# Shifts and scales of the first two quarters as products with w_ada as the stationary operand, and a new order of the first stage

## The chip, the cores and the metric

The kernel runs on one core of a Trainium2 chip, as one program. The metric is the device time of one execution in microseconds. Before the change it is 1251.24 us, the median of 3 runs (1251.12 to 1252.87). Engines go by the profile's names: PE (TensorE's matmuls), PEld (its weight loads), DVE (VectorE), ACT (ScalarE), POOL (GpSimd) and SP (SyncE, which issues most DMAs here).

## The reference, cut to what matters

One layer of a streaming encoder on 1024 prompt tokens and 32 sample tokens, D = 1024 channels. The first stage of the kernel computes this part:

```python
mod = jax.nn.silu(c) @ w_ada + b_ada            # c: one vector for the prompt, one for the samples
shift, scale, gate = jnp.split(mod, 3, axis=-1) # w_ada is 1024 x 3072
h = rms_norm(x, g_norm) * (1 + scale[:, None, :]) + shift[:, None, :]
z = h @ w_in                                    # all projections, 1024 x 8264
q, k, v, gate_a, iq, iw, ik, glu, gate_b, merge = split_in(z)
```

Behind it come an indexer that picks the top keys for each query, attention over those, a causal depthwise convolution of width 31, two output projections with gates, a last projection and a final norm. All of it is float32; the big products are made of three products of rounded halves (high x high, high x low, low x high).

## The kernel before, in words

The kernel runs through stages. The first one, which the change touches, makes h transposed: tiles hh and hl hold its high and low halves, with channels on partitions (8 blocks of 128 channels, j = 0 to 7) and 1056 tokens along the free axis. Beside it the stage computes the first index products: ik (the index keys and weights, 72 columns, in three pieces of 352 tokens: steps k:j,c) and the first 128 columns of iq (in two pieces, 512 and 288 tokens: steps q:j,c). When it ends, the projections follow (line 543 in helper proj, and the second iq product from line 132 on), 24 matmuls for each 128 columns and third of the tokens, which fill most of the span.

What the stage does in what order is written out by hand. LOADS lists the DMAs on SP's queue: x:i is token tile i (8 is the sample tile), a:g,h a block of w_ada for quarter g and half h of the rows (512 rows x 512 columns: the shifts and scales of two blocks of channels), k and q:0, q:1 the index weights. Tile pools limit them: three buffers for blocks of w_ada ("ada", line 228), six for x. A load that reuses a buffer waits on SP until its readers are done, and everything behind it in SP's queue waits too.

ORDER lists the steps of the compute engines; each engine goes through its own steps in this order. A last letter names the engine (D, P, A for DVE, POOL, ACT).

- sq, v, s, r, x: the norm of a token tile: sum of squares (ACT), variance (DVE), root (ACT), reciprocal and a correction (DVE), scaling of the tile in place
- t:i,q and c:i,q: four transposes of 128x128 on PE into a PSUM tile (misc, two buffers), and the copy to xT
- m:g,h (mod, line 339): products with a block of w_ada. Four matmuls; the stationary operand is the pair of vectors (padded to 32 columns), the 512 columns of w_ada move. The four go to four quarters of the output partitions: each has a fourth of the half's rows, and all accumulate over h
- a:g (mod_row, line 348): the PSUM tile is copied to SBUF; o:g (mod_cols, line 353): four transposes turn its rows to columns; O:g (mod_out, line 358): a reduce on DVE adds the four quarters, and bias and norm weight go on. After O:g the shifts and scales of blocks 2g and 2g + 1 stand in AB
- h:p,j, i:p,j, l:p,j: for part p of the tokens (f is tiles 0 and 1, i is 2 to 5, t is 6 and 7, tf is f and t) h in full, its high half (ACT) and the low half as their difference (DVE); S:g the same for the sample tokens
- wa, wd: the high and low halves of the index weights
- z:n: n matmuls of zeros, which fill PE's waiting time

Buffers and queues hold the steps together: mod of group 1 needs the blocks loaded into buffers that mod of group 0 has freed, and an index product of block j needs its h, which needs O of its quarter and the transposes of its tokens.

Of the kernel before, what the change touches and what calls it, by code (L numbers as in the profile page):

```python
# [24 lines left out]
OP = mybir.AluOpType  # L25
# [5 lines left out]
D = 1024  # L31
# [41 lines left out]
def steps(text):  # L73
    return [(op, *(int(v) if v.isdigit() else v for v in args.split(",") if v))
            for op, _, args in (word.partition(":") for word in text.split())]
# [3 lines left out]
x:8 x:2 x:3 x:4 x:5 a:0,0 a:0,1 k x:6 x:7 a:1,0 a:1,1 q:0 a:2,0 a:2,1 x:0 x:1 a:3,0 a:3,1 q:1  # L79
""")  # L80
ORDER = steps("""
sq:8 v:8 s:8 B sq:3 r:8 x:8,D s:3 sq:4 z:8 t:8,1 t:8,0 c:8,1,D v:3 c:8,0,D s:4 v:4 sq:5 r:4 x:4,D s:5 r:3 sq:2 z:5
t:4,0 v:5 t:4,1 x:3,P r:5 m:0,0 c:4,0,D s:2 c:4,1,A x:5,P v:2 t:3,0 r:2 c:3,0,A x:2,D z:1 t:5,1 t:2,0 c:5,1,D wa:k
c:2,0,D t:2,1 wd:k,P m:0,1 c:2,1,D sq:6 t:3,1 t:5,0 v:6 s:6 sq:7 r:6 a:0,D x:6,P s:7 v:7 c:3,1,A r:7 c:5,0,A z:5 o:0
O:0 t:6,1 c:6,1,A S:0,D h:i,0,P t:6,0 m:1,0 i:i,0 h:i,1,D x:7,P i:i,1 l:i,0 m:1,1 c:6,0,D l:i,1 k:0,1 wa:0 a:1,D
t:7,1 t:7,0 c:7,1,A wd:0,P k:1,1 c:7,0,A o:1 i:t,0 h:t,1,D O:1 m:2,0 i:t,1 h:t,0,D i:i,3 l:t,0 h:t,2,P q:0,0 l:t,1
h:i,2,P i:t,2 h:i,3,D k:0,2 i:i,2 l:i,3 q:1,1 S:1,P k:1,2 i:t,3 l:i,2 q:1,0 m:2,1 sq:0 q:3,0 s:0 v:0 sq:1 r:0 k:3,1
a:2,D x:0,P q:2,0 v:1 s:1 k:2,1 r:1 o:2 x:1,P t:0,0 O:2 m:3,0 c:0,0,A l:t,2 i:i,5 h:i,5,D S:2,P h:t,3,D t:1,0 i:i,4
l:t,3 t:0,1 c:1,0,D k:2,2 c:0,1,A m:3,1 l:i,5 h:i,4,P i:f,2 i:f,1 q:3,1 a:3,D h:f,3,P i:f,0 t:1,1 l:i,4 k:5,1 h:f,2,P
c:1,1,A q:5,0 i:tf,4 h:tf,4,D h:tf,5,P o:3 l:f,2 i:tf,5 k:4,1 O:3 k:2,0 S:3,P i:i,6 l:tf,5 q:4,0 i:i,7 l:tf,4 q:0,1  # L90
k:3,2 i:tf,7 q:2,1 k:5,0 i:f,3 k:5,2 i:tf,6 l:f,3 q:5,1 h:i,7,D k:4,2 h:i,6,P wa:1 k:4,0 l:i,7 q:4,1 h:tf,6,P l:i,6
k:3,0 q:7,0 h:f,0,P l:tf,6 q:6,0 wd:1,P l:f,0 k:7,1 h:tf,7,D k:6,0 l:tf,7 q:6,1 k:6,1 q:7,1 h:f,1,P k:7,0 k:7,2 l:f,1
k:0,0 k:6,2 k:1,0
""")

GROUPS = ((0, 2), (2, 2), (4, 2), (6, 2))


def pieces(n):
# [10 lines left out]
def _build(tc, nc, a, o, top):  # L110
# [10 lines left out]
    def tl(p, shape, dt, tag, bufs=1):  # L121
        return p.tile(shape, dt, name=tag, tag=tag, bufs=bufs)
# [49 lines left out]
    def misc(shape):  # L172
        return tl(psM, shape, F, "misc", 2)
# [48 lines left out]
    ada = {}  # L222
    xn = {}

    def load_ada(g, h):

        f, n = GROUPS[g]
        t = ada[g, h] = tl(stp, [128, 4, 512], F, "ada", 3)[:, :, :256 * n].rearrange("p k (i c) -> p k i c", i=2)
# [12 lines left out]
    for op, *i in LOADS:  # L241
# [6 lines left out]
        else:  # L248
            c = 128 * i[0]
# [16 lines left out]
    scp = tl(stp, [128, KD, 32], F, "scp")  # L266
# [70 lines left out]
    pm, mrow = {}, {}  # L337

    def mod(g, h):

        w = 256 * GROUPS[g][1]
        if h == 0:
            pm[g] = tl(psS, [128, 512], F, "acc")
        for j in range(4):
            nc.tensor.matmul(pm[g][32 * j:32 * j + 32, :w], scp[:, 4 * h + j, :],
                             ada[g, h][:, j].rearrange("p i c -> p (i c)"), start=h == 0, stop=h == 1)

    def mod_row(g, e):
        w = 256 * GROUPS[g][1]
        mrow[g] = tl(stp, [128, 512], F, "mrow")[:, :w]  # L350
        copy_on(e, mrow[g], pm.pop(g)[:, :w])

    def mod_cols(g):
        p = pm[g] = misc([128, 4, 128])
        for c in range(2 * GROUPS[g][1]):
            nc.tensor.transpose(p[:, c, :], mrow[g][:, 128 * c:128 * c + 128], ident)

    def mod_out(g):

        f, n = GROUPS[g]  # L360
        j = slice(f, f + n)
        mc = tl(stp, [128, 4, 2], F, "mc", 2)[:, :2 * n]
        nc.vector.tensor_reduce(out=mc, in_=pm.pop(g)[:, :2 * n].rearrange("p c (q s) -> p c s q", q=4)[:, :, 0:2],
                                axis=mybir.AxisListType.X, op=OP.add)
        bias = bg_[:, 0:16].rearrange("p (i j) -> p i j", i=2)[:, :, j, None]
        nc.vector.tensor_add(AB[:, j].rearrange("p j (i s) -> p i j s", i=2), mc.rearrange("p (i j) s -> p i j s", i=2),
                             bias.to_broadcast([128, 2, n, 2]))
        nc.vector.tensor_mul(AB[:, j, 2:4], AB[:, j, 2:4], bg_[:, 16:24][:, j, None].to_broadcast([128, n, 2]))
# [73 lines left out]
    def idle(n):  # L442

        for i in range(n):
            nc.tensor.matmul(ikp[:, 0, :], rest[:, 0:128], rest, start=True, stop=True)

    order = {"sq": sq_x, "v": var_x, "s": root_x, "r": over_x, "x": scale_x, "t": trans_x, "c": copy_x, "m": mod,
             "a": mod_row, "o": mod_cols, "O": mod_out, "h": h_of, "i": h_hi, "l": h_lo, "S": h_sample, "wa": w_hi,
             "wd": w_lo, "B": bias_out,
             "q": q_mm, "k": k_mm, "z": idle}  # L450
# [420 lines left out]
    def spill(dst, func):  # L871
        def f(j):
            def g(p):
                s = slot()
                nc.scalar.activation(c3(s[:, :T]), p[:, :, :CH], func)  # L875
                nc.scalar.dma_start(dst[128 * j:128 * j + 128, :], s[:, :T])
            return g
        return f
# [177 lines left out]
    def pairs(w, c0, f, rows):  # L1056
        return [("w", [(w, c0 + 128 * j, 256)], [(0, 128, f(j)), (128, 128, f(j + 1))], 1, rows)
                for j in range(0, KD, 2)]
# [225 lines left out]
    sq = [(u, r) for u in units for r in range(u.ns)]  # L1284
# [37 lines left out]
    def prelude():  # L1322
        more_q(1)
        more_g(2)
        for _ in range(8):
# [8 lines left out]
    m = (pairs(w_in, C_MA, spill(sma_d, AF.Sigmoid), hrows) + pairs(w_in, C_MB, spill(smb_d, AF.Sigmoid), hrows)  # L1334
         + pairs(w_in, C_GA, spill(ga_d, AF.Silu), hrows) + pairs(w_in, C_Q, spill_q, hrows))
# [111 lines left out]
    start = {}  # L1447
# [262 lines left out]
def _layout(x):  # L1710
# [10 lines left out]
    w = x["w_ada"][0]  # L1721
    for g, (f, n) in enumerate(GROUPS):
        for h in range(2):
# [25 lines left out]
```

## Time and profile before

| | us |
|---|---|
| time, median of 3 runs | 1251.24 (1251.12 to 1252.87) |
| the profiled execution's own time | 1251.41 |
| its span, from the first instruction to the last | 1249.6 |
| first stage, to the first projection's first matmul | 57.78 |
| last matmul | 1239.5 |

The span begins with the first instruction and the profile's times count from there. A row of a timeline gives start, length, engine, line, operation, output <- inputs, shapes and number of instructions merged, and in brackets the idle time before and what ended it. Matmuls of float32 operands appear as two records each; transposes and the matmuls of rounded halves as one. A chain of waits is followed back from the end, at each step to what released it.

### The profile page before, as it was taken

The page shows a single profiled execution, that of the slowest core. Times are in us where ns is not written, and L with a number is a line of the kernel's source. Part 1 is how long each engine was busy: PE and PEld are TensorE (multiplying, and loading weights), DVE is VectorE, ACT ScalarE, POOL GpSimd, SP SyncE. Part 2 cuts the span into 40 slices and gives each one's busy share as a digit, 9 for nine tenths or more (in the row PEclk, how much of TensorE's full clock was granted, in tenths as well). Part 3 has the DMA queues.
Part 4 walks back from the last instruction along what each step waited for, and adds up shares of the span by engine and source line. Part 5 has one row for each costly group of instructions (what it writes and reads, how often), then busy time and mean ns, then how long its engine had stood idle before and what let it go on. Part 6 is the DMA issues. An engine that isn't in the chain of part 4 may idle for free.

```text
span 1249.6 us, 18980 instructions
## 1 busy us (share of the span) xinstructions
PE 1229.2 (98%) x7403; PEld 1167.6 (93%) x7403; DVE 894.1 (72%) x1413; ACT 605.2 (48%) x1115; POOL 180.6 (14%) x279
## 2 busy tenths in 40 slices
PE   7999999999999999999999999999999999999996
PEld 3799999999999999999999999999998889999785
DVE  6766538988899888888876469752358888775464
ACT  6645545675666666671214343340247776123321
POOL 4610010000000000100000000000123352200343
PEclk8999999999999999999999999999999999999999
DMA  9412232213213113113223421276123336645422
GB/s 362 168 43 69 85 88 84 70 54 94 79 53 86 69 53 120 53 52 104 86 91 134 160 80 52 88 240 210 40 88 100 98 89 196 211 148 184 159 88 86
DMA packets 107898, 137.94 MB, mean 110 GB/s; under 512 B 9280, under 2 KB 88384, under 8 KB 106656
## 3 DMA queue, kind: packets, MB, share of 16 engines
q1 hardware_dynamic: 97136, 102.88, 25.9%
q10 hardware_dynamic: 5808, 19.06, 3.8%
q0 software_dynamic: 4864, 14.79, 3.6%
q8 instruction: 58, 0.95, 0.3%
q14 instruction: 32, 0.26, 0.1%
HBM read 100.43 MB, written 36.27 MB: 109 GB/s over the span
## 4 chain that ended last, share of the span: by engine, by line
PE 96%; DMA 1%; DVE 1%; ACT 0%; POOL 0%; issue 0%; SPq 0%; POOLq 0%; ACTq 0%
PE proj L543 70%; PE PT L1250 2%; PE y L132 2%; PE y L133 2%; PE y L134 2%; PE O L132 1%; PE O L134 1%; PE O L133 1%; PE misc L712 1%; PE misc L713 1%; PE misc L134 1%; PE misc L133 1%; PE misc L132 1%; DMA ada<-in_ada_dram 1%; PE proj L132 1%; PE proj L134 1%
## 5 line engine op out<-in xcount | busy, mean ns | idle before, releaser
L931 DVE SCALAR_TENSOR_TENSOR s<-u,vec,s 128x1086 f32<-128x1086 f32 x240 | 314.3, 1346 | 2.9
L543 PE MATMUL proj<-hl,wh 128*128 128x352 f32 x1440 | 311.6, 324 | 0.0
L543 PE MATMUL proj<-hh,wh 128*128 128x352 f32 x1440 | 311.3, 324 | 0.0
L543 PE MATMUL proj<-hh,wl 128*128 128x352 f32 x1440 | 309.0, 323 | 0.0
L543 PEld LDWEIGHTS proj<-hh,wh 128*128 128x128 f32 x1440 | 244.8, 188 | 1.6
L543 PEld LDWEIGHTS proj<-hh,wl 128*128 128x128 f32 x1440 | 246.0, 188 | 0.0
L543 PEld LDWEIGHTS proj<-hl,wh 128*128 128x128 f32 x1440 | 245.0, 188 | 0.0
L782 ACT ACTIVATE relu<-scores,cand 128x384 bf16<-128x384 f32 (+6 forms) x224 | 183.6, 821 | 82.2 <-DVE cand L797 78.5
L129 DVE TENSOR_TENSOR wl<-raw,wh 128x1024 fp32r<-128x1024 f32 (+1 forms) x82 | 97.8, 1195 | 71.1 <-ACT wh L128 71.0
L128 ACT CAST wh<-raw 128x1024 fp32r<-128x1024 f32 (+1 forms) x82 | 83.8, 1025 | 61.4 <-PE proj L543 49.3
L726 DVE SCALAR_TENSOR_TENSOR scores<-relu,iws,scores 128x384 f32<-128x384 f32 (+3 forms) x70 | 43.1, 655 | 31.6 <-ACT relu L715 31.5
L715 ACT ACTIVATE relu<-misc 128x384 f32<-128x384 f32 (+3 forms) x80 | 39.7, 523 | 52.4 <-PE misc L713 49.8
L128 ACT CAST u<-PT 128x512 fp32r<-128x512 f32 (+2 forms) x76 | 43.2, 572 | 44.5 <-PE PT L1250 42.2
L875 ACT ACTIVATE s<-proj 128x1056 f32<-128x1056 f32 x24 | 25.3, 1054 | 78.2 <-PE proj L543 78.2
L129 DVE TENSOR_TENSOR u<-PT,u 128x512 fp32r<-128x512 f32 (+2 forms) x76 | 50.6, 670 | 14.5 <-ACT u L128 14.2
L782 ACT ACTIVATION_READ_ACCUMULATOR relu<-scores,cand 128x1 f32 x224 | 42.0, 188 | 0.0
L543 PE MATMUL proj<-oa,wh 128*128 128x352 f32 x192 | 41.4, 323 | 0.0
L1230 POOL TENSOR_SCALAR E<-E,st 128x1024 f32<-128x1024 f32 (+4 forms) x36 | 33.6, 935 | 41.8 <-DVE st L1229 18.6
L543 PE MATMUL proj<-u,wh 128*128 128x352 f32 x192 | 38.7, 323 | 0.0
L1225 ACT ACTIVATE E<-E,st 128x1024 f32<-128x1024 f32 (+4 forms) x36 | 34.7, 963 | 8.1 <-DVE st L1218 7.9
L857 POOL DMA_DIRECT2D mask_d<-relu x7 | 3.8, 540 | 232.1 <-ACT relu L856 232.1
L885 DVE TENSOR_TENSOR s<-proj,s 128x1056 fp32r<-128x1056 f32 x8 | 10.1, 1256 | 35.6 <-ACT s L883 35.6
(400 smaller groups left out, 2052.1 us busy)
## 6 DMA issues: line engine op xcount, KB each, us to landing
raw<-in_w_in_dram SPq DMA_DIRECT2D x23, 1024.0 KB, 5.4
ada<-in_ada_dram SPq DMA_DIRECT2D x8, 1024.0 KB, 9.2
raw<-in_w_in_dram SPq DMA_DIRECT2D x16, 512.0 KB, 4.8
raw<-in_w_out_dram SPq DMA_DIRECT2D x6, 1024.0 KB, 5.4
sma_d<-s ACTq DMA_DIRECT2D x8, 528.0 KB, 2.7
smb_d<-s ACTq DMA_DIRECT2D x8, 528.0 KB, 2.8
ga_d<-s ACTq DMA_DIRECT2D x8, 528.0 KB, 2.7
qh_d<-s ACTq DMA_DIRECT2D x8, 528.0 KB, 2.7
```

The costliest lines, as they stand in the source:

```text
L128: nc.scalar.copy(hi, src)
L129: nc.vector.tensor_sub(lo, src, f32(hi))
L132: nc.tensor.matmul(out, ah, bh, start=first, stop=False)
L133: nc.tensor.matmul(out, ah, bl, start=False, stop=False)
L134: nc.tensor.matmul(out, al, bh, start=False, stop=last)
L543: nc.tensor.matmul(p[:n, c, :CH], a_[:, k, :n], b_(k, c), start=first, stop=last)
L715: nc.scalar.activation(r[:, :n], p[:, :n], AF.Relu, scale=0.125)
L726: nc.vector.scalar_tensor_tensor(acc, r[:, :n], w, acc, op0=OP.mult, op1=OP.add)
L782: nc.scalar.activation(scr[:, :s.shape[1]], s, AF.Sign, bias=f32(hold["cand"])[:, i:i + 1], accum_out=cnt[:, i:i + 1])
L931: nc.vector.scalar_tensor_tensor(d[:, :DW], u[:, k:k + DW], wj[:, k:k + 1], d[:, :DW], op0=OP.mult, op1=OP.add)
L1225: nc.scalar.activation(e, e, AF.Exp, bias=mn, scale=-1.0, accum_out=st[:, 1:2])
L1230: nc.gpsimd.tensor_scalar(e, e, st[:, 2:3], 1.0, op0=OP.mult, op1=OP.mult)
```

## The change

For groups 0 and 1 (TURNED) the product is turned: each 128x128 tile of the block of w_ada becomes the stationary operand, and the two vectors, two columns, move. The result is columns at once, so that a:0, a:1, o:0 and o:1 are not needed; O reduces over the two halves h in place of the four quarters. Groups 2 and 3 stay as they were. ORDER is written anew for the whole stage (a:2, a:3 and some of the copies go to ACT, tile 8's scaling to POOL, fewer fill matmuls); LOADS stays.

```diff
@@ ORDER @@
-sq:8 v:8 s:8 B sq:3 r:8 x:8,D s:3 sq:4 z:8 t:8,1 t:8,0 c:8,1,D v:3 c:8,0,D s:4 v:4 sq:5 r:4 x:4,D s:5 r:3 sq:2 z:5
-t:4,0 v:5 t:4,1 x:3,P r:5 m:0,0 c:4,0,D s:2 c:4,1,A x:5,P v:2 t:3,0 r:2 c:3,0,A x:2,D z:1 t:5,1 t:2,0 c:5,1,D wa:k
-c:2,0,D t:2,1 wd:k,P m:0,1 c:2,1,D sq:6 t:3,1 t:5,0 v:6 s:6 sq:7 r:6 a:0,D x:6,P s:7 v:7 c:3,1,A r:7 c:5,0,A z:5 o:0
-O:0 t:6,1 c:6,1,A S:0,D h:i,0,P t:6,0 m:1,0 i:i,0 h:i,1,D x:7,P i:i,1 l:i,0 m:1,1 c:6,0,D l:i,1 k:0,1 wa:0 a:1,D
-t:7,1 t:7,0 c:7,1,A wd:0,P k:1,1 c:7,0,A o:1 i:t,0 h:t,1,D O:1 m:2,0 i:t,1 h:t,0,D i:i,3 l:t,0 h:t,2,P q:0,0 l:t,1
...
-k:3,0 q:7,0 h:f,0,P l:tf,6 q:6,0 wd:1,P l:f,0 k:7,1 h:tf,7,D k:6,0 l:tf,7 q:6,1 k:6,1 q:7,1 h:f,1,P k:7,0 k:7,2 l:f,1
-k:0,0 k:6,2 k:1,0
+B sq:8 v:8 s:8 sq:3 r:8 x:8,P v:3 s:3 sq:2 r:3 z:9 t:8,0 x:3,P t:8,1 c:8,0,D s:2 v:2 c:8,1,A r:2 sq:5 z:1 t:3,1 x:2,P
+t:3,0 s:5 v:5 c:3,1,A m:0,0 r:5 sq:4 c:3,0,D x:5,D t:2,1 s:4 t:2,0 c:2,1,D m:0,1 c:2,0,A v:4 r:4 wa:k x:4,P t:5,1
+sq:6 O:0 t:5,0 wd:k,D S:0,P c:5,1,A v:6 c:5,0,D s:6 z:2 t:4,0 sq:7 r:6 t:4,1 x:6,P s:7 v:7 c:4,1,D c:4,0,A z:2 m:1,0
+h:i,0,D i:i,1 r:7 i:i,0 x:7,P t:6,0 l:i,0 t:6,1 c:6,0,A h:i,1,D m:1,1 c:6,1,A l:i,1 wa:0 t:7,1 O:1 wd:0,P t:7,0
+c:7,1,A S:1,D k:0,1 i:i,3 k:1,1 h:i,3,D i:i,2 m:2,0 c:7,0,A h:i,2,P q:0,0 i:t,3 q:1,0 i:t,0 h:t,0,P l:i,2 i:t,2 m:2,1
+h:t,3,P l:t,0 i:t,1 l:i,3 q:2,0 a:2,A sq:0 k:2,1 h:t,1,D h:t,2,P o:2 l:t,1 q:0,1 s:0 v:0 k:0,2 l:t,2 sq:1 k:3,1 r:0
+q:1,1 q:3,0 x:0,P s:1 v:1 O:2 q:2,1 r:1 k:2,2 i:i,4 h:i,4,P m:3,0 x:1,D i:i,5 S:2,P l:i,4 t:0,1 c:0,1,A m:3,1 l:t,3
...
+h:f,2,P l:f,3 q:7,0 i:f,0 k:7,2 i:f,2 l:f,0 h:f,1,P k:6,2 l:f,2 q:6,1 wd:1,P l:f,1 k:0,0 k:2,0 k:3,0 k:6,0 k:1,0
+k:7,1 k:4,1
+TURNED = (0, 1)
@@ mod @@
-        w = 256 * GROUPS[g][1]
+        n = GROUPS[g][1]
+        w = 256 * n
         if h == 0:
             pm[g] = tl(psS, [128, 512], F, "acc")
+        if g in TURNED:
+
+            for c in range(2 * n):
+                z = 4 * n * h + 2 * c
+                for j in range(4):
+                    nc.tensor.matmul(pm[g][:, z:z + 2], ada[g, h][:, j, c // n, 128 * (c % n):128 * (c % n) + 128],
+                                     scp[:, 4 * h + j, 0:2], start=j == 0, stop=j == 3)
+            return
@@ mod_out @@
-        nc.vector.tensor_reduce(out=mc, in_=pm.pop(g)[:, :2 * n].rearrange("p c (q s) -> p c s q", q=4)[:, :, 0:2],
-                                axis=mybir.AxisListType.X, op=OP.add)
+        p = pm.pop(g)
+        if g in TURNED:
+            p = p[:, :8 * n].rearrange("p (h c s) -> p c s h", h=2, c=2 * n)
+        else:
+            p = p[:, :2 * n].rearrange("p c (q s) -> p c s q", q=4)[:, :, 0:2]
+        nc.vector.tensor_reduce(out=mc, in_=p, axis=mybir.AxisListType.X, op=OP.add)
```

## Rows read from the trace of the kernel before

**Rows 1.** The page: span and instructions; busy time and share of each engine.
```profile
span 1249.6 us, 18980 instructions
...
PE 1229.2 (98%) x7403; PEld 1167.6 (93%) x7403; DVE 894.1 (72%) x1413; ACT 605.2 (48%) x1115; POOL 180.6 (14%) x279
```

**Rows 2.** Busy time by stretch; the first row names the columns.
```profile
core 0: us, PE busy (x) PEld busy (x) DVE busy (x) ACT busy (x) POOL busy (x), PEclk, DMA share, GB/s
...
12.20:29.43 17.23, 15.44 (x101) 8.77 (x101) 14.26 (x37) 11.80 (x22) 9.38 (x7) 0.91 1.04 391
29.43:57.78 28.35, 26.95 (x170) 20.09 (x171) 23.86 (x50) 17.80 (x30) 22.09 (x29) 1.00 0.59 209
57.78:1239.50 1181.72, 1180.95 (x7112) 1136.72 (x7112) 848.99 (x1302) 565.97 (x1043) 144.14 (x213) 1.00 0.32 102
```

**Rows 3.** The chain of waits, first 62 us: start, us, what.
```profile
19.48 9.90 DMA ada<-in_ada_dram
...
29.43 1.06 PE acc L345 x8
...
39.87 0.16 PE ik L132
...
50.93 2.61 DVE hl L390
...
54.03 0.78 DVE hl L390
...
57.79 0.46 PE proj L132
```

**Rows 4.** PE's waits from 29.5 to 57.78 us: us in total, times, longest.
```profile
PE iq L133 <- DVE hl L390: 1.4, 1, 1.4
```

**Rows 5.** Timeline of PE, 12 to 22 us.
```profile
12.23 1.94 PE L331 MATMUL misc<-ident,xt 128*128 128x128 f32 x8 [2.88 <-DVE rs_r L310]
...
18.35 1.06 PE L345 MATMUL acc<-ada,scp 128*32 128x512 f32 x8
19.35 1.09 PE L331 MATMUL misc<-ident,xt 128*128 128x128 f32 x8
20.28 1.24 PE L445 MATMUL ik<-rest 128*128 128x512 bf16 x5
```

**Rows 6.** Timeline of all engines, 8 to 14 us.
```profile
8.94 0.29 ACT L304 ACTIVATE rs_s<-ss,eps 128x1 f32<-128x1 f32 x1
...
10.63 0.16 DVE L310 RECIPROCAL rs_r<-rs_s 128x1 f32<-128x1 f32 x1 [0.17 <-ACT rs_s L304]
...
11.27 0.81 DVE L322 TENSOR_SCALAR xt<-xt,rs_r,rs_t 128x1024 f32<-128x1024 f32 x1
...
12.79 2.38 POOL L322 TENSOR_SCALAR xt<-xt,rs_r,rs_t 128x1024 f32<-128x1024 f32 x2 [8.82 <-DVE rs_r L310]
```

**Rows 7.** Timeline of PE around line 998.
```profile
701.09 1.99 PE L998 MATMUL misc<-ones,s 128*128 128x2 f32 x18
703.02 0.75 PE L543 MATMUL proj<-hh,wh 128*128 128x352 f32 x3
```

**Rows 8.** Busy time by stretch, as rows 2; granted clock third from the end.
```profile
5.07:8.48 3.41, 1.33 (x12) 0.96 (x13) 1.81 (x7) 1.12 (x4) 0.00 (x0) 1.00 1.03 417
8.48:15.31 6.83, 3.96 (x19) 1.78 (x17) 4.69 (x19) 5.30 (x13) 2.38 (x2) 0.50 1.05 401
15.31:57.78 42.47, 39.31 (x258) 27.09 (x255) 35.36 (x76) 27.92 (x48) 29.09 (x34) 1.00 0.74 272
```

**Rows 9.** Timeline of SP's queue: pairs of DMA issues, held up included.
```profile
19.48 4.80 SPq L229 DMA_DIRECT2D ada<-in_ada_dram  x2
...
25.34 5.54 SPq L229 DMA_DIRECT2D ada<-in_ada_dram  x2
```

**Rows 10.** The page's DMA issues: count, KB each, us to landing.
```profile
raw<-in_w_in_dram SPq DMA_DIRECT2D x23, 1024.0 KB, 5.4
```

**Rows 11.** Timeline of POOL, end of the first stage.
```profile
50.86 2.39 POOL L439 TENSOR_TENSOR wl<-raw,wh 128x1024 fp32r<-128x1024 f32 x1
```

More of the change, by code (lines that the diff above doesn't have):

```diff
@@ L87 @@
[L87 to L91, printed above, removed]
@@ new lines @@
+c:7,1,A S:1,D k:0,1 i:i,3 k:1,1 h:i,3,D i:i,2 m:2,0 c:7,0,A h:i,2,P q:0,0 i:t,3 q:1,0 i:t,0 h:t,0,P l:i,2 i:t,2 m:2,1
+h:t,3,P l:t,0 i:t,1 l:i,3 q:2,0 a:2,A sq:0 k:2,1 h:t,1,D h:t,2,P o:2 l:t,1 q:0,1 s:0 v:0 k:0,2 l:t,2 sq:1 k:3,1 r:0
+q:1,1 q:3,0 x:0,P s:1 v:1 O:2 q:2,1 r:1 k:2,2 i:i,4 h:i,4,P m:3,0 x:1,D i:i,5 S:2,P l:i,4 t:0,1 c:0,1,A m:3,1 l:t,3
+h:i,5,D t:1,1 a:3,A l:i,5 k:1,2 c:1,1,A q:4,0 i:tf,4 h:tf,5,P h:tf,4,D o:3 t:0,0 i:tf,5 l:tf,4 k:5,1 c:0,0,A O:3
+q:3,1 k:3,2 i:i,7 h:i,6,D S:3,P q:5,0 l:tf,5 k:4,2 i:tf,7 q:4,1 h:tf,7,D i:i,6 t:1,0 l:tf,7 k:4,0 h:i,7,P i:tf,6
@@ L94 @@
+k:5,0 l:i,6 q:5,1 wa:1 h:tf,6,P q:7,1 l:i,7 k:5,2 c:1,0,A k:6,1 l:tf,6 q:6,0 h:f,3,P i:f,3 h:f,0,D i:f,1 k:7,0
+h:f,2,P l:f,3 q:7,0 i:f,0 k:7,2 i:f,2 l:f,0 h:f,1,P k:6,2 l:f,2 q:6,1 wd:1,P l:f,1 k:0,0 k:2,0 k:3,0 k:6,0 k:1,0
+k:7,1 k:4,1
 """)
 GROUPS = ((0, 2), (2, 2), (4, 2), (6, 2))
+TURNED = (0, 1)
 def pieces(n):
```

## The prediction

> **What bounds the kernel now.** I read the page's totals first, then busy time by stretch, then the chain of waits of the first 62 us, then the timelines of single engines there. The page: TensorE (PE) has matmuls under way in 98% of a span of 1249.6 us [rows 1]. By stretch, nothing is left to gain or absorb behind the first stage: from 57.78 us, where the first projection starts, to the last matmul at 1239.5, PE is idle for 0.77 us of 1181.7 [rows 2]. So whatever the first stage ends earlier or later, the span does too, one for one; the change touches that stage alone.
>
> The first stage has two halves. Up to 29.43 us it is bound by the loads of w_ada: the chain runs through a DMA of 9.9 us that started at 19.48 and released the first product of group 2 at 29.43 [rows 3]. In the 17.2 us before, PE was idle for 1.8 us, and the DMA engines were busy throughout (share 1.04) [rows 2]. From 29.43 to 57.78 PE itself is the bound: 26.95 of 28.35 us busy [rows 2], and the missing 1.4 us are one wait, for a low half of h [rows 4]: VectorE took 2.61 us for a subtraction of 256 columns and came late to the next [rows 3], in the time in which GpSimd split the weights of q [rows 11].
>
> **The change part by part.** *The products.* A call m:g,h of groups 0 and 1 has four matmuls now, with the narrow vectors as stationary operand and 512 columns moving; their eight records take 1.06 us at the full clock [rows 5]. After the change a call has 4 chunks x 4 rows of blocks = 16 matmuls with a 128x128 float32 tile of w_ada as stationary operand and two columns moving. The kernel before has just that operation once, far behind: the channel sums at line 998, 9 matmuls in 18 records, because a float32 matmul stands as two records. From their first at 701.09 to the next line's first at 703.02 are 1.93 us [rows 7], 0.107 us a record, with a weight load in each. Hence 16 x 2 x 0.107 = 3.4 us a call; two of the 18 records are narrow (one tile of 32 columns), so that a wide one costs up to 1.93/16 = 0.12, and a call up to 3.9. I take 3.5. The bounds from farther rows: not under the 1.06 of today's call [rows 5], and not over 7.0, should the clock be at half.
>
> The Trainium skill has a rule that would make it far cheaper: in "TensorE: Matmul & The Clock Gate", section "Wait — 56ns, not 53.3ns?", the start-to-start time of small matmuls has a floor of about 25 ns. By that alone a call would be 32 x 25 ns = 0.8 us (an estimate from the page). The rows at line 998 show 107 ns, so they decide; what the rule would give is the first rival.
>
> *What goes.* The row copies a:0 and a:1 (VectorE) and the transposes o:0 and o:1 (PE) go; the fill matmuls behind the first full tile's transposes fall from six to four, at 0.22 us each (five of them in 1.24 us with the last one's drain [rows 5]). None of the VectorE time counts: VectorE is on the path only at 50.93 to 54.8.
>
> *The first half, counted anew on PE.* First tile: its root starts on ScalarE at 8.94 and takes 0.29; from reciprocal to scaling VectorE needs 0.64 (10.63 to 11.27), and GpSimd scales in 1.19 (two in 2.38) [rows 6]: 8.94 + 0.29 + 0.64 + 1.19 = 11.1, so the transposes of tile 3 start at 11.2 instead of 12.23 (those of tile 4 now) [rows 5]. The granted clock is half from 8.48 to 15.31 and full after that [rows 8]. I keep that, since PE comes to work about as early as now. Then, in the new order: tile 3 at half clock 1.9 (to 13.1); m:0,0 with 2.2 us at half clock, worth 1.1, and 2.4 more (to 17.7); tiles 2, 5, 4, 6 and 7 at 1.0 each (eight transposes took 1.09 [rows 5]) 5.0; m:0,1, m:1,0, m:1,1 at 3.5, 10.5; four fills 0.9; two k pieces of three matmuls at 0.16 [rows 3] 1.0. That is 17.7 + 17.4 = 35.1: the first product of group 2 starts at 35.1 instead of 29.43, 5.7 later.
>
> *Do the loads still hide?* A load of w_ada goes out when the product that frees its buffer ends, and SP's queue stands behind it: pairs of issues ended at 24.28 and 30.88, each held up for this [rows 9]. Now the calls end later: m:0,1 at 22.2 (19.4 before), so ada 2,0 goes out 2.7 later. A 1 MB load that meets no queue lands after 5.4 us [rows 10], so it is there by 29.4 at the latest, well ahead of 35.1. m:1,0 ends at 28.6 and frees ada 2,1, m:1,1 at 33.1 ada 3,0, m:2,0 at 36.2 ada 3,1: they land by 34.0, 39 and 41.6. With 0.16 for a matmul of 352 columns [rows 3] and so 0.23 for one of 512, the new order wants them at about 37.6, 43.5 and 45. The x tiles 0 and 1, which stand in SP's queue behind ada 2,1, land about 2 us later than now and are wanted at 44.6. So the loads no longer bind; the smallest cover is the 3 us of the last one. If it were gone, the end would move by the lack.
>
> *The second half.* From the first product of group 2 on, PE's instructions are the same ones in another order: 26.95 us. The wait of 1.4 us has a reason to go: the split of the last q weights (2.39 us on GpSimd [rows 11]) now stands behind all of GpSimd's h pieces, not before the last of them, and the other engines have some 5 us more lead. What is late next is the subtraction l:f,1, which has that split beside it; it is wanted 1.4 us before the end, by my count with under 1 us to spare; lost cover costs up to 1. So from 29.43 the stage took 28.35, from 35.1 it takes 26.95: it ends at 62.0 instead of 57.78, +4.2. For small waits in the packed first half, where PE had 1.8 us of idle time, I add 0.3: **+4.5**.
>
> *The sum.* The profiled execution took 1251.41 us, 1.81 over its span; 1251.4 + 4.5 = 1255.9. It lies 0.17 over the median of the runs shown (1251.24), so I forecast 1255.7. Its own range is 1254 to 1258: at the one end 3.4 a call (-0.4), no small waits (-0.3) and a clock that rises earlier; at the other 3.9 a call (+1.5) and one of two waits, the 1.4 us or a late l:f,1.
>
> **The rivals.** *Cheap products (not slower).* If a weight load runs beside the matmul before it, a record costs less than the 0.107: of a transpose, whose eight take 1.09, the load can be half, 0.07, and the sum is 2.2 a call: four calls save 3 x 1.3 + 1.3 = 5.2 against 3.5 each, and PE reaches group 2 at 29.9, about when the load of ada 2,0 lets it now. Then only the 1.4 us wait can go, and the time is 1249.8 (the load binds at 29.43) to 1251.7 (at 29.9, and the wait stays). For it: loads run ahead of matmuls in the projections, where they cost nothing. Against it: at line 998 they don't, with the same types and shapes. It can't come much below 1249.8, since behind 29.4 stand 26.95 us of PE work.
>
> *The half clock (slower still).* The calls stream two columns at a time. If that doesn't count as work for the clock, it stays at 1.2 GHz, its lower level, through the calls. For it: between 5.07 and 8.48 PE had records under way for 1.33 of 3.41 us and the clock was lowered right after [rows 8]. Against it: at line 998 the clock was full, but only for 2 us between dense work. Priced: a call at half clock is 7.0; with the first two so, 2.4 + 3.5 = +5.9, 1261.6; with all four, +12.9, 1268.6, and the late loads would add to it. The Trainium skill bears on this: "TensorE: Matmul & The Clock Gate", section "Part 4: PE-mode transpose", says that transposes don't bring up the full clock the way matmuls do. By that the transposes between the calls would not help, and the dear end is the likelier one; in the trace the clock rose at 15.31 behind transposes and products both, so it doesn't tell them apart.
>
> **How the numbers follow.** The forecast 0.60, the half clock 0.23, cheap products 0.12, something not seen 0.05. The range, 1250 to 1267, holds the forecast, most of cheap products and all but the dearest half-clock cases. Differences under 0.2% (2.5 us) can't be told from none here: 1248.7 to 1253.7. Faster by more needs both halves to gain, which no count above allows: 0.05. Within: cheap products and the rim of the forecast, 0.17. Slower 0.78.
>
> **What would show it.** Right: 32 records a call, some 0.11 us apart; group 2's first product near 35 with no wait for its load; no PE wait for a low half of h near the end; first projection near 62. Wrong: records closer than 0.07; a wait for ada 2,0 at about 29; granted clock of half beyond 15.3 or a new dip before 35; a first projection before 58.

## The result: slower by 1.5%, 1271 us, with the clock at half through three of the four turned calls

The changed kernel takes 1270.97 us (median of 4 runs, 1268.48 to 1271.17) against 1252.05 (median of 4, 1251.12 to 1252.90) for the kernel before on the same chip: a ratio of 1.0147, 95% interval 1.0135 to 1.0159. The forecast was 1255.7 with a range of 1250 to 1267; the time lies outside it, on the side of the rival that was called the half clock.

The page after, the lines that answer to [rows 1]:

```profile
span 1269.3 us, 19144 instructions
...
PE 1251.4 (99%) x7486; PEld 1194.6 (94%) x7486; DVE 889.7 (70%) x1406; ACT 607.4 (48%) x1120; POOL 180.7 (14%) x279
```

PE is busier than before, in share and in time. Read alone, this line would say that PE got 22 us more work; in truth much of it is the same work at half the clock. Busy time by stretch, as in [rows 2], the three stretches being PE's work up to group 2, from there to the first projection, and the rest:

```profile
10.98:48.64 37.66, 37.66 (x186) 36.06 (x186) 13.26 (x37) 13.88 (x26) 9.59 (x10) 0.55 0.68 245
48.64:77.49 28.85, 27.84 (x171) 19.84 (x171) 22.24 (x45) 19.48 (x34) 19.78 (x25) 0.98 0.43 140
77.49:1259.50 1182.01, 1180.89 (x7112) 1136.82 (x7112) 849.12 (x1303) 565.28 (x1043) 143.98 (x213) 1.00 0.31 102
```

The rest is what it was (1182.0 against 1181.7), so the whole difference is in the first stage: its end moved from 57.78 to 77.49, by 19.7, and the profiled executions differ by 1271.17 - 1251.41 = 19.8. The first stretch did it: group 2 starts at 48.64 instead of 29.43, 19.2 later, with PE busy all the time and a mean granted clock of 0.55. The DMA engines, at 1.04 in [rows 2], fall to 0.68: the loads now wait for PE (SP's queue stood 29.8 us in all behind the turned products). By the granted clock (third column from the end), as in [rows 8]:

```profile
5.36:8.77 3.41, 1.00 (x9) 0.67 (x9) 0.77 (x5) 1.58 (x4) 1.92 (x5) 1.00 1.03 398
8.77:32.67 23.90, 21.69 (x100) 20.82 (x101) 7.71 (x31) 10.43 (x23) 6.37 (x8) 0.50 0.83 305
32.67:36.08 3.41, 3.41 (x32) 3.38 (x30) 3.31 (x8) 1.02 (x2) 1.70 (x1) 1.00 0.00 0
36.08:49.73 13.65, 13.65 (x66) 12.06 (x65) 4.82 (x10) 5.67 (x10) 3.80 (x3) 0.50 0.64 233
```

Before, half clock ended at 15.31 for good. Now it lasts to 32.67, ends there for a moment, and comes back until 49.73, although PE is never idle between 10.98 and 49.73. The timeline of PE tells what ran in each stretch; it answers to [rows 5]:

```profile
10.98 1.97 PE L333 MATMUL misc<-ident,xt 128*128 128x128 f32 x8 [2.23 <-DVE rs_t L313]
12.74 6.83 PE L352 MATMUL acc<-scp,ada 128*128 128x2 f32 x32
19.43 1.95 PE L333 MATMUL misc<-ident,xt 128*128 128x128 f32 x8
21.17 6.83 PE L352 MATMUL acc<-scp,ada 128*128 128x2 f32 x32
27.86 1.95 PE L333 MATMUL misc<-ident,xt 128*128 128x128 f32 x8
29.60 1.06 PE L460 MATMUL ik<-rest 128*128 128x512 bf16 x2
30.45 1.91 PE L333 MATMUL misc<-ident,xt 128*128 128x128 f32 x8
32.16 0.85 PE L460 MATMUL ik<-rest 128*128 128x512 bf16 x2
32.84 3.87 PE L352 MATMUL acc<-scp,ada 128*128 128x2 f32 x32
36.58 1.95 PE L333 MATMUL misc<-ident,xt 128*128 128x128 f32 x8
38.32 6.83 PE L352 MATMUL acc<-scp,ada 128*128 128x2 f32 x32
45.01 1.95 PE L333 MATMUL misc<-ident,xt 128*128 128x128 f32 x8
```

L352 is the turned product. A call has 32 records, as forecast; three calls take 6.7 us from their first record to the next line's, and the one from 32.84 to 36.58 takes 3.7. That third call began right after a stretch of transposes and fills, at whose end the clock had risen; the clock fell again at 36.08, before the call was over. Where the 13.8 us between the forecast 23.9 (11.2 to 35.1) and the measured 37.7 went: m:0,1 and m:1,1 3.2 each over 3.5, m:0,0 2.1 over 4.6, m:1,0 0.2, and 5.1 for what stands between the calls at half clock: the transposes of five tiles took 8.5 instead of 5.0, the k pieces 2.0 instead of 1.0, the fills 1.5 instead of 0.9.

### The profile page after: what moved, and what is told of

It reads as the page before. It is cut to its first block, busy times and chain, and to the rows that moved or that the text cites. A ratio compares the mean times of both kernels' runs of the same rounds, so it can differ in the third digit from the quotient of the medians.

```text
span 1269.3 us, 19144 instructions
## 1 busy us (share of the span) xinstructions
PE 1251.4 (99%) x7486; PEld 1194.6 (94%) x7486; DVE 889.7 (70%) x1406; ACT 607.4 (48%) x1120; POOL 180.7 (14%) x279
## 4 chain that ended last, share of the span: by engine, by line
PE 97%; POOL 1%; DVE 1%; ACT 1%; DMA 0%; issue 0%; SPq 0%; POOLq 0%; ACTq 0%; DVEq 0%
PE proj L558 69%; PE PT L1265 2%; PE y L134 2%; PE y L135 2%; PE y L136 2%; PE acc L352 2%; PE O L134 1%; PE O L136 1%; PE O L135 1%; PE misc L727 1%; PE misc L728 1%; PE misc L136 1%; PE misc L135 1%; PE misc L134 1%; PE misc L333 1%; PE proj L134 1%
```

## Experiments

Theories. *Clock*: products with two moving columns don't bring the granted clock up and don't hold it, and everything in their stretch runs at 1.2 GHz. *Order*: the new order, with fewer fills, lets the clock fall. *Length*: the calls are long whatever the clock. Ratios are against the kernel before on the same chip (1251.3 to 1251.4 in its medians there).

**Order alone.** The new order, with the products of before:

```diff
-TURNED = (0, 1)
+TURNED = ()
 ORDER: a:0,D behind m:0,1; o:0 ahead of O:0; a:1,D behind m:1,1; o:1 ahead of O:1
        c:5,1,A and c:7,1,A moved ahead, to O:0 and O:1
```

> The new order with the four-matmul products of before in all groups (a:0, a:1, o:0, o:1 put back into it). Clock theory (the two-column products keep the granted clock at half): no such product is left, so the clock rises at about 15 us and stays; the first product of group 2 starts at 29 to 30, released by its load, the first projection at 56 to 58, time 1250 to 1252.5. Order theory (the new order with fewer fills lets the clock fall): half clock until about 30, group 2 not before 33, time 1255 or more. Length theory (the products are long whatever the clock): as the clock theory here.

Measured: 1251.77 us (10 runs, 1251.11 to 1252.70), ratio 0.9997, interval 0.9987 to 1.0006; first projection at 58.35. Clock by stretch, as above:

```profile
8.58:15.41 6.83, 4.07 (x18) 2.04 (x18) 3.95 (x15) 5.58 (x14) 2.39 (x2) 0.50 1.04 407
15.41:58.35 42.94, 38.87 (x253) 26.32 (x252) 34.10 (x76) 30.32 (x53) 27.56 (x33) 1.00 0.74 271
```

The clock rises at 15.41 and stays, as before. The order costs nothing that can be measured and gives nothing; the order theory falls. The first projection is later than the 56 to 58 expected, though group 2 starts at 29.17: from there the new order takes 29.2 us in place of 28.35, 1.7 of them waits. More on that below.

**Products alone.** The order of before, with the turned products:

```diff
 ORDER of before
-... a:0,D ... o:0 ... a:1,D ... o:1 ...
+TURNED = (0, 1), mod and mod_out as changed
```

> The order of before with the turned products of groups 0 and 1 (only a:0, a:1, o:0, o:1 taken out). Clock theory: half clock through most of the first 45 us, calls of 6.6 us, group 2 at 45 to 50, time 1265 to 1273. Order theory: clock full from about 15, calls of 3.5, group 2 at 34 to 36, time 1255 to 1258. Length theory: calls of 6.6 us at either clock, 1265 to 1273 with a full clock in the records.

Measured: 1271.64 us (2 runs, 1269.86 and 1273.41), ratio 1.0156, interval 1.0125 to 1.0187. PE's timeline:

```profile
14.05 6.83 PE L352 MATMUL acc<-scp,ada 128*128 128x2 f32 x32
...
24.81 6.83 PE L352 MATMUL acc<-scp,ada 128*128 128x2 f32 x32
...
36.84 10.77 PE L352 MATMUL acc<-scp,ada 128*128 128x2 f32 x64
```

The whole loss comes with the products, in an order that has five more fills. The last two calls stand back to back here; the clock is full from 36.59 and falls at 40.00, inside them, with PE busy throughout. This profile's records of the granted clock begin only at 36.59, so its mean clock of 0.994 says nothing of the time ahead of that; the records' distance does: 32 in 6.83 us is the half clock's.

**Fills between the products.** One matmul of zeros behind every four turned ones:

```diff
                     nc.tensor.matmul(pm[g][:, z:z + 2], ..., scp[:, 4 * h + j, 0:2], start=j == 0, stop=j == 3)
+                idle(1)
             return
```

> The changed kernel with one matmul of zeros (512 columns) behind every four turned matmuls, 16 fills more. Clock theory: full clock from about 15; a call is 3.5 us plus four fills of 0.22, 4.4 us; group 2 at 37.5 to 39.5, first projection at 64.5 to 66.5, time 1258 to 1261, some 11 us under the changed kernel although PE has more to do. Length theory: calls of 6.6 plus 0.9, group 2 at 50 or more, 1272 to 1276. Order theory: the fills mend the clock too, so it is told apart by the two kernels above.

Measured: 1271.75 us (4 runs, 1268.72 to 1275.85), ratio 1.0167, interval 1.0133 to 1.0201: no mending, a miss for my numbers. The four times are two pairs, 1268.7 and 1268.8, and 1274.7 and 1275.9; the profile is of the first pair, and what the second did isn't shown. In the profiled execution the first two calls stay at half clock (7.8 us each with their fills); the last two run at the full one (4.1):

```profile
12.85 1.71 PE L352 MATMUL acc<-scp,ada 128*128 128x2 f32 x8
14.41 0.59 PE L461 MATMUL ik<-rest 128*128 128x512 bf16 x1
...
34.11 0.95 PE L352 MATMUL acc<-scp,ada 128*128 128x2 f32 x8
34.92 0.38 PE L461 MATMUL ik<-rest 128*128 128x512 bf16 x1
```

```profile
32.91:43.15 10.24, 10.24 (x90) 9.78 (x90) 4.57 (x12) 4.55 (x9) 3.07 (x2) 1.00 0.50 186
```

Eight records take 1.56 us at the one clock and 0.81 at the other, which settles the length theory. So sparse fills did not lift the clock here; once it was up, it stayed up through two calls with them (32.91 to 43.15), and fell as the second ended.

**64 moving columns.** The same products, with two used columns and 62 of zeros:

```diff
-    scp = tl(stp, [128, KD, 32], F, "scp")
+    scp = tl(stp, [128, KD, 64], F, "scp")
-                z = 4 * n * h + 2 * c
+                z = 64 * (2 * n * h + c)
-                    nc.tensor.matmul(pm[g][:, z:z + 2], ..., scp[:, 4 * h + j, 0:2], ...)
+                    nc.tensor.matmul(pm[g][:, z:z + 64], ..., scp[:, 4 * h + j, :], ...)
 ... (the products of groups 2 and 3 take scp's first 32 columns, the reduce its first two)
```

> The changed kernel with 64 moving columns in a turned product (two used, the rest zeros), no instruction more. If what counts for the clock is columns streamed: full clock from about 15, calls of 3.5 (columns hidden under the weight loads) to 5.2 us (columns added to them), group 2 at 35 to 42, time 1255.5 to 1262. If the clock goes by matmuls or weight loads issued, whatever their width: half clock as in the changed kernel, calls of 6.6 us or more, 1271 or more.

Measured: 1263.87 us (2 runs), ratio 1.0094, interval 1.0068 to 1.0120: between the two expectations. The first two calls are at half clock by their length; the last two are at the full one, and the clock, whose records begin at 30.26 here, doesn't fall any more before PE's work ends:

```profile
12.88 6.93 PE L352 MATMUL acc<-scp,ada 128*128 128x64 f32 x32
...
21.31 6.93 PE L352 MATMUL acc<-scp,ada 128*128 128x64 f32 x32
...
31.73 3.68 PE L352 MATMUL acc<-scp,ada 128*128 128x64 f32 x32
35.25 1.05 PE L333 MATMUL misc<-ident,xt 128*128 128x128 f32 x8
36.13 3.68 PE L352 MATMUL acc<-scp,ada 128*128 128x64 f32 x32
```

Two things follow. 64 columns cost next to no time over two: a call at half clock takes 6.72 us (12.88 to 19.60) and 6.69 with two; at the full one it takes 3.52 (31.73 to 35.25), 0.110 a record. So they hide under the weight loads. And matmuls and loads are as many as in the changed kernel, where the clock fell in the third call; here it did not, and the columns that a product moves are what differs.

**A warm start, with 64 columns and with two.** PE's idle time ahead of the first products is filled:

```diff
-... z:9 t:8,0 ... z:1 t:3,1 ...
+... z:16 t:8,0 ... z:9 t:3,1 ...
```

> As the kernel with 64 moving columns, and PE's idle time ahead of the first products filled with matmuls of zeros (z:9 to z:16, z:1 to z:9), so that the clock is up when m:0,0 starts. This times the forecast's own case, a full clock throughout. Clock theory: calls of 3.5 us all four, group 2 at 33 to 35, first projection at 60 to 62, time 1253.5 to 1256. If wide columns hold the clock only in some places: one or two calls at half clock, 1258 to 1264. If the forecast's sum lacks a term (late loads, a wait at the end), a full clock and still over 1257.

> The changed kernel (two columns) with the same fills ahead of the first products. Clock theory: the clock is full when m:0,0 starts and falls in it or right behind it; m:0,1 at half clock, 6.6 us; time 1264 to 1271. If the changed kernel only lacked a warm start: full clock in all four calls, 1253.5 to 1256 as with 64 columns.

With 64 columns: 1255.60 us (5 runs, 1255.52 to 1256.38), ratio 1.0031, interval 1.0019 to 1.0043. Full clock from 6.64 on, four calls of 3.5 to 3.6, first projection at 62.0:

```profile
12.66 3.79 PE L352 MATMUL acc<-scp,ada 128*128 128x64 f32 x32 [0.45 <-DMA ada<-in_ada_dram]
...
17.16 3.69 PE L352 MATMUL acc<-scp,ada 128*128 128x64 f32 x32
...
23.77 3.68 PE L352 MATMUL acc<-scp,ada 128*128 128x64 f32 x32
...
28.17 3.68 PE L352 MATMUL acc<-scp,ada 128*128 128x64 f32 x32
```

```profile
6.64:62.00 55.36, 52.80 (x377) 41.93 (x376) 35.07 (x89) 36.47 (x67) 31.70 (x40) 1.00 0.76 274
33.63:62.00 28.37, 27.32 (x171) 19.82 (x171) 21.72 (x46) 20.65 (x37) 18.53 (x24) 1.00 0.55 183
```

This is the forecast's case, made by hand, and the forecast's time (1255.7). With two columns: 1269.95 us (2 runs), ratio 1.0143, interval 1.0125 to 1.0162. PE's first and third call and the clock by stretch:

```profile
12.69 5.32 PE L352 MATMUL acc<-scp,ada 128*128 128x2 f32 x32 [0.43 <-DMA ada<-in_ada_dram]
...
31.44 3.72 PE L352 MATMUL acc<-scp,ada 128*128 128x2 f32 x32
35.02 1.95 PE L333 MATMUL misc<-ident,xt 128*128 128x128 f32 x8
```

```profile
4.31:14.55 10.24, 7.71 (x52) 4.78 (x49) 4.51 (x19) 7.50 (x17) 4.31 (x7) 1.00 1.02 409
14.55:31.62 17.07, 17.07 (x79) 16.11 (x78) 4.42 (x17) 5.92 (x12) 3.99 (x6) 0.50 0.80 289
```

It is full when m:0,0 starts at 12.69 and falls at 14.55, in the middle of the call, with PE busy without a break since 12.69. The wait of 0.43 ahead of it is no cause: with 64 columns it is 0.45, and the clock stays. One edit, 64 columns for two, is worth 14.3 us here.

**No fills around tile 4's transposes.**

```diff
-... c:5,0,D s:6 z:2 t:4,0 ... c:4,0,A z:2 m:1,0
+... c:5,0,D s:6 t:4,0 ... c:4,0,A m:1,0
```

> The changed kernel without the two z:2 around the transposes of tile 4, so that between m:0,1 and m:1,0 stand transposes alone, some 3.5 us at half clock. If transposes bring the clock up as matmuls do: it rises at 30 to 33 as in the changed kernel, m:1,0 at 3.5 to 4.5 us, 1268 to 1272. If they don't (the skill's rule): half clock through m:1,0 and m:1,1, 6.6 us each, the rise not before the index products at 48, 1272 to 1276.

Measured: 1269.89 us (2 runs, 1269.75 and 1270.03), ratio 1.0143, interval 1.0124 to 1.0161; the changed kernel's 1.0147 lies in it. PE's timeline and the clock:

```profile
27.98 3.61 PE L333 MATMUL misc<-ident,xt 128*128 128x128 f32 x16
31.42 3.92 PE L352 MATMUL acc<-scp,ada 128*128 128x2 f32 x32
```

```profile
7.31:31.20 23.89, 21.70 (x104) 20.66 (x105) 7.55 (x30) 10.58 (x24) 6.13 (x12) 0.50 0.84 314
31.20:34.61 3.41, 3.41 (x33) 3.41 (x32) 2.91 (x9) 2.04 (x4) 2.22 (x2) 1.00 0.30 127
```

From 27.98 to 31.42 PE ran transposes alone, and the clock rose at 31.20. So transposes bring it up here, without the fills; whether these cost time, two runs don't tell.

**The wait near the end: the split moved, and the split on VectorE.** Both are edits of the kernel before, made for its wait of 1.4 us [rows 4]. The first:

```diff
-... q:6,0 wd:1,P l:f,0 ... h:f,1,P k:7,0 ...
+... q:6,0 l:f,0 ... h:f,1,P wd:1,P k:7,0 ...
```

> The kernel before with one step moved: the split of the last q weights on GpSimd (wd:1) behind the last h piece (h:f,1). If PE's wait of 1.4 us near the end comes from that split: the wait goes or falls under 0.4, the first projection starts at 56.4 to 57.0, time 0.8 to 1.4 under before (ratio 0.9989 to 0.9994). If l:f,1 or another low half is late anyway: within 0.3 of before.

Measured: 1251.33 us, ratio 0.9997 (0.9988 to 1.0006), and the wait still 1.4. It tells nothing of the wait, since GpSimd did not follow: its split ran at 50.93, ahead of the last h piece, as before. Unlike what the description of the kernel says of each engine, ORDER sets the order on PE, VectorE and ScalarE alone (manual_schedule in the kernel names these three); GpSimd's is left to the program that builds the kernel. The second edit leaves it no split to place:

```diff
-... q:6,0 wd:1,P l:f,0 ...
+... q:6,0 wd:1,D l:f,0 ...
```

> The kernel before with the split of the last q weights (wd:1) on VectorE, in the same place of the order, so that GpSimd has only h pieces there. If PE's wait of 1.4 us near the end comes from GpSimd's split, which VectorE's subtraction of 2.6 us stood beside: that subtraction falls to 0.4 to 0.7, the split costs VectorE 1.2 to 1.4, the wait falls to 0.8 or less, the first projection starts at 56.6 to 57.3, time 0.4 to 1.2 under before. If VectorE was slow there for another reason: the subtraction keeps its 2.6, the wait is longer by the 1.2, time 0.5 to 1.5 over before.

Measured: 1250.18 us (11 runs, 1249.95 to 1253.93) against 1251.32, ratio 0.9995, interval 0.9986 to 1.0004: by medians 1.1 faster, but the interval holds one. The profile is clear: PE's wait falls to 0.2, the first projection starts at 56.55, and VectorE's subtraction, 2.61 us in [rows 3], takes 0.41 right behind its own split of 1.41:

```profile
50.46 1.41 DVE L439 TENSOR_TENSOR wl<-raw,wh 128x1024 fp32r<-128x1024 f32 x1
51.79 0.41 DVE L390 TENSOR_TENSOR hl<-h,hh 128x256 fp32r<-128x256 f32 x1
```

So VectorE had been slow because GpSimd's split ran beside it. In what way the one slows the other, no run here shows.

**The kernel before, warm.** More fills there too, and both edits together:

```diff
-... sq:4 z:8 t:8,1 ... sq:2 z:5 t:4,0 ...
+... sq:4 z:15 t:8,1 ... sq:2 z:11 t:4,0 ...
```

> The kernel before with more matmuls of zeros ahead of the first products (z:8 to z:15, z:5 to z:11), 13 in all. Load theory of the first half (group 2 waits for its load at 29.4): a full clock from 5 to 7 on, and still group 2 at 29.2 to 29.6, time as before within 0.8. If PE at half clock was on the path ahead of it: group 2 at 27.5 to 28.5, time 1 to 2 under before. Executions of before near 1254 (mean clock 0.992) should be gone.

> Both of these edits of the kernel before together. If each does what its theory says: first projection at 56.6 to 57.3, 1250.0 to 1250.9, no execution near 1254, and so under both the kernel before and the changed one, by 0.4 to 1.2 against before's usual executions. If the split on VectorE doesn't help: as the kernel before, 1251 to 1252.5.

Warm alone: 1251.37 us, ratio 0.9999 (0.9990 to 1.0008). The clock is full from 4.07 on, and group 2 still starts at 29.24, after a wait of 1.33 for its load: the loads bound the first half, as read.

```profile
29.24 1.07 PE L345 MATMUL acc<-ada,scp 128*32 128x512 f32 x8 [1.33 <-DMA ada<-in_ada_dram]
```

Three of the eleven executions were still at 1252.0 to 1253.9, so that expectation did not hold in full. Both edits: 1250.36 us (11 runs, 1249.90 to 1250.84), ratio 0.9987, interval 0.9978 to 0.9996. It is the one version whose interval lies below the kernel before, if only by 0.13%; by median the split alone was 0.2 us lower still, so which of the two is faster isn't shown.

## Why the prediction was wrong

The step that failed stands in the first half's count: "The granted clock is half from 8.48 to 15.31 and full after that. I keep that, since PE comes to work about as early as now." When PE starts to work was the wrong thing to ask. The turned products themselves decide: with two columns they let a full clock fall in mid-call (14.55, two columns and a warm start), and with 64 they hold it. So three calls took 6.7 us where the count has 3.5 to 4.6, and what stands between them ran at half clock too: 13.8 us of the 15.3 by which the time missed the forecast. This was the second rival, at a chance of 0.23, and its dear end was left out of the range.

Point by point:

- *3.5 us a call at full clock*: right. 3.5 to 3.6 in all four with 64 columns and a warm start, and 3.6 in the third call of the warm version with two columns (31.44 to 35.02), which had the full clock from 31.62 to its end. The rows of line 998 were the right ones for the price of the operation, and not for its clock: there 2 us of it stood between dense work [rows 7].
- *Four fills 0.9, tiles at 1.0, k pieces 1.0*: right at full clock. In the kernel with 64 columns and a warm start PE's stretch from tile 3 to group 2 took 22.5 us; the forecast's 23.9 less the 2.0 that a full clock saves on tile 3 and m:0,0 is 21.9.
- *The loads no longer bind*: right, by the waits of PE after, which name none; the warm version with 64 columns has one, 0.45, ahead of the first call. Nor did the later loads add to the half clock's price, as that rival had it.
- *The 1.4 us wait goes*: half right, for a wrong reason. PE's waits from group 2 on in the changed kernel:

```profile
PE proj L134 <- DVE s L541: 0.5, 1, 0.5
PE ik L135 <- DVE hl L405: 0.5, 2, 0.3
```

They are 1.0 in place of 1.4, and the 0.5 for line 541 is new: the first projection now waits for VectorE, a wait that the count doesn't have. The new order alone has the same waits. The split had not gone behind the h pieces: GpSimd ran it at 68.92, with three pieces behind it, and VectorE's subtraction beside it took 2.89:

```profile
68.92 2.40 POOL L454 TENSOR_TENSOR wl<-raw,wh 128x1024 fp32r<-128x1024 f32 x1
71.31 3.01 POOL L399 TENSOR_SCALAR h<-xT,AB 128x256 f32<-128x256 f32 x3
```

```profile
68.98 2.89 DVE L405 TENSOR_TENSOR hl<-h,hh 128x512 fp32r<-128x512 f32 x1 [0.51 <-POOL h L399]
```

- *The sum at full clock, 1255.7*: the warm version with 64 columns took 1255.6, though two errors cancelled in it: its first half was 1.5 us shorter than my count (the clock was up earlier) and its second, 28.4, was 1.4 longer than the 26.95 that I took, 1.0 of it those waits and 0.4 PE's own time (27.32 busy). That the sum came out is luck in this part.
- *Cheap products*: did not come. A record took 0.110 us at full clock with 64 columns (3.52 a call) and 0.112 with two (3.58), where this rival needed 0.07.
- *The half clock's price*: 1268.6 was near by luck, made of the wrong parts. I priced four calls at half clock, 12.9 us; the calls lost 8.7, and what I left out, the transposes, k pieces and fills between them at half clock, 5.1. The rest of the 2.4 us over that price is mostly the second half, 28.85 where I had 26.95.
- *The rule on transposes* (the Trainium skill, "TensorE: Matmul & The Clock Gate", section "Part 4: PE-mode transpose"), that they don't bring up the full clock as matmuls do: the run without fills shows the opposite in this kernel, a rise at 31.20, 3.2 us into transposes alone. By the rule the transposes between the calls would not have helped; they did, and most of one of the four calls ran at full clock for it.

What stays open: why the first two calls stay at half clock with 64 columns, and with sparse fills, while later the same mixture keeps a full clock, with 64 columns for good and with fills through two calls. The runs show that rising and holding differ, not what makes the difference.

## What to carry to other kernels

A matmul that is mostly weight load has two prices: its own, which a row of the same operation gives, and the clock that it leaves to all that stands near it, which a short row between dense work doesn't give. Before turning a product so that the wide operand is stationary, count what streams, and if it is a column or two, time it with the moving side padded: 62 columns of zeros were free here, and worth 7 us as the kernel stood and 14 with a warm start. Padding mends the clock and not the change: at full clock a turned call is still 3.5 us in place of 1.06, and the best turned version is 4.2 us over the kernel before. And when PE's busy share rises, read the granted clock beside it before calling it work.

## What the runs showed of the hardware that was not expected

- The clock fell with PE busy without a break: at 14.55 in the warm version with two columns, at 36.08 in the changed kernel and at 40.00 with the products alone, each time inside a turned call with two columns.
- At half clock the turned products' records lie 0.209 us apart, at the full one 0.112. Their time hardly depends on the columns that move, so it is the weight loads, too, that go at the granted clock.
- Padding two moving columns to 64 took no time that shows: a call took 6.72 us in place of 6.69 at half clock, 3.52 in place of 3.58 at the full one.
- Transposes alone brought the clock up: 3.2 us of them, from 27.98 to the rise at 31.20.
- VectorE's subtraction of 256 columns took 2.61 us beside GpSimd's split and 0.41 without it.
